# Softmax in sixteen-row tiles: three big buffers, one short buffer, and a changed order of divide and maximum

## The chip, the cores and the metric

The kernel runs on one core of a Trainium2 chip. The metric is the device time of one execution in microseconds; for the kernel before it is the median of 3 runs, 317.07 us (317.07 to 317.11). The core has several engines that run their own instruction streams and wait for each other by semaphores. Three of them matter here: the vector engine (DVE) for maxima and divisions, the scalar engine (ACT) for exponentials, and the transfers between main memory (HBM) and on-chip memory (SBUF), which 16 DMA engines carry. A transfer is issued by an instruction on one of three queues: SP's, POOL's (GpSimd's) or ACT's. SBUF has 128 partitions; a tile is a block of it, partitions by columns.

## The reference

A softmax with a temperature over the last axis of a 32 x 512 x 1024 float32 array; the temperature is 0.5.

```python
scaled = x / temperature
shifted = scaled - np.max(scaled, axis=-1, keepdims=True)
exp_x = np.exp(shifted)
return exp_x / np.sum(exp_x, axis=-1, keepdims=True)
```

There are 16,384 rows of 1024 numbers. With 128 partitions, that is 128 rows for each partition. In this text "a row" of a tile means one row of 1024 numbers in every partition: 128 x 4 KB, 0.524 MB. The whole task is 128 such rows in and 128 such rows out.

## The kernel before

A tile holds k consecutive rows in every partition and is loaded by one DMA, worked on in place and written back by one DMA from the same buffer. `PASSES` (line 10) lists the tiles, and in each tile the groups of rows that are worked on together: tile 0 has 12 rows in groups of 4, tiles 1 to 9 have 12 rows in groups of 6, tile 10 has 8 rows in groups of 4. The pool `data` has `BUFS` = 4 buffers of 12 rows (48 KB in each partition), so tile i uses the buffer of tile i-4.

A group is handled in three steps.

- `maximum` (lines 63 to 72): DVE reduces the group to one maximum for each row (L69) and scales it to a bias (L72).
- `exponential` (lines 74 to 85): ACT computes exp(scale * x + bias) row by row (L78), and each instruction also sums up its row.
- `divide` (lines 87 to 98): DVE takes the reciprocals of the sums (L90) and multiplies the group, either with one instruction on the whole group (L93, tiles 2, 3, 4, 6 and 8) or with one instruction for each row (L96, the other tiles).

`store` (lines 100 to 109) does something only after the last group of a tile: it issues the tile's store, on POOL's queue for tiles 0 to 5 and on ACT's for tiles 6 to 10, and then `load` issues the next load on SP's queue. That load waits until the store that last used its buffer has landed. Before the first store, POOL copies one number out of tile 2 (L106), so this store is not issued until tile 2 has been loaded.

The order on the engines is written by hand (lines 113 to 128). Four loads are issued first. Then, for each group g, the maximum and the exponentials of g come before the division of group g-1, so that ACT works while DVE divides the group before. This holds across tiles too: the last group of a tile is divided after the first maximum of the next tile. Only from tile 9 on (`ALONE`) does a tile's first group come after the division and the store of the tile before.

Of the kernel before, what the change touches and what calls it, by code (L numbers as in the profile page):

```python
# [1 line left out]

# [4 lines left out]

PASSES = [[4, 4, 4]] + [[6, 6]] * 9 + [[4, 4]]  # L10
BUFS = 4

WHOLE = (2, 3, 4, 6, 8)


BY_POOL = 6

ALONE = 9


@with_exitstack
def kernel(
    ctx: ExitStack,
    tc: tile.TileContext,
    x: bass.AP,
    temperature: bass.AP,
    out: bass.AP,
):
    nc = tc.nc
    f32 = mybir.dt.float32  # L30
    scale = 1.0 / float(temperature)
    extreme = mybir.AluOpType.max if scale > 0 else mybir.AluOpType.min

    P = 128
    xf = x.flatten_outer_dims()
    of = out.flatten_outer_dims()
    n, d = xf.shape
    rows = [sum(ks) for ks in PASSES]
    assert sum(rows) * P == n

    data = ctx.enter_context(tc.tile_pool(name="data", bufs=BUFS))
    stats = ctx.enter_context(tc.tile_pool(name="stats", bufs=4))


    groups = []
    for i, ks in enumerate(PASSES):
        for j, k in enumerate(ks):
            groups.append((i, sum(ks[:j]), k))

    def dram(t, i):  # L50
        block = t[P * sum(rows[:i]) : P * sum(rows[: i + 1]), :]
        return block.rearrange("(p k) d -> p k d", p=P, k=rows[i])

    tiles, small = [], []

    def load():
        i = len(tiles)
        if i < len(PASSES):
            xt = data.tile([P, rows[i], d], f32, name="xt")
            nc.sync.dma_start(out=xt, in_=dram(xf, i))  # L60
            tiles.append(xt)

    def maximum(g):
        i, a, k = groups[g]
        top, bias, sums, recip = (
            stats.tile([P, k], f32, name=name) for name in ("top", "bias", "sums", "recip")
        )
        small.append((bias, sums, recip))
        nc.vector.tensor_reduce(  # L69
            out=top, in_=tiles[i][:, a : a + k, :], axis=mybir.AxisListType.X, op=extreme  # L70
        )
        nc.vector.tensor_scalar_mul(bias, in0=top, scalar1=-scale)  # L72

    def exponential(g):
        i, a, k = groups[g]
        bias, sums, _ = small[g]
        for b in range(k):
            nc.scalar.activation(  # L78
                tiles[i][:, a + b, :],
                tiles[i][:, a + b, :],  # L80
                mybir.ActivationFunctionType.Exp,
                bias=bias[:, b : b + 1],
                scale=scale,
                accum_out=sums[:, b : b + 1],
            )

    def divide(g):
        i, a, k = groups[g]
        _, sums, recip = small[g]
        nc.vector.reciprocal(recip, sums)  # L90
        if i in WHOLE:
            xt = tiles[i][:, a : a + k, :]
            nc.vector.tensor_mul(xt, xt, recip.unsqueeze(2).to_broadcast([P, k, d]))  # L93
            return
        for b in range(k):
            nc.vector.tensor_scalar_mul(  # L96
                tiles[i][:, a + b, :], in0=tiles[i][:, a + b, :], scalar1=recip[:, b : b + 1]
            )

    def store(g):  # L100
        i, a, k = groups[g]
        if a + k == rows[i]:
            if i == 0:


                nc.gpsimd.tensor_copy(stats.tile([P, 1], f32, name="seen"), tiles[2][:, 0, 0:1])  # L106
            queue = nc.gpsimd if i < BY_POOL else nc.scalar
            queue.dma_start(out=dram(of, i), in_=tiles[i])  # L108
            load()

    with tc.manual_schedule():
        for _ in range(BUFS):
            load()
        for g in range(len(groups) + 1):

            alone = g < len(groups) and groups[g][0] >= ALONE and groups[g][1] == 0
            if g > 0 and alone:
                divide(g - 1)  # L120
                store(g - 1)
            if g < len(groups):
                maximum(g)
                exponential(g)
            if g > 0 and not alone:
                divide(g - 1)
                store(g - 1)


# [1 line left out]
_INS = ['x', 'temperature']  # L131
_OUTS = [((32, 512, 1024), 'float32')]

_NUMBERS = {'temperature': 0.5}


# [26 lines left out]
```

## Time and profile before

| what | value |
|---|---|
| median of 3 runs | 317.07 us |
| the profiled execution: its span | 315.8 us |
| DVE busy | 256.9 us (81%) |
| ACT busy | 148.3 us (47%) |
| POOL busy | 3.7 us (1%) |
| bytes read from and written to HBM | 67.11 MB each |
| mean rate over the span | 425 GB/s |
| loads: median time from issue to landing, 12 rows | 36.4 us |
| stores on POOL's queue, the same | 35.9 us |

The profile is of one execution. The span runs from the first to the last instruction that the profiler recorded; the device time holds a little more, 1.3 us here by the median. In groups of the profile, "L69" is the source line, "128x6 f32<-128x6144 f32" the output and input of one instruction (partitions by numbers), "x18" how often it ran; then come the total busy time, the mean of one in ns, and the idle time of the engine just before these instructions with what ended it. A DMA has two moments that matter: its issue on a queue, and its landing, when its semaphore tells the waiting engines that all bytes have arrived.

### The profile page before, as it was taken

To read this page: it belongs to the slowest core of one execution; us is meant where nothing else is said; L and a number is where in the kernel's file an instruction comes from. 1 tells how busy PE (TensorE), PEld (TensorE's weight loads), DVE (VectorE), ACT (ScalarE), POOL (GpSimd) and SP (SyncE) were. 2 spreads that over 40 slices of the span, in tenths; PEclk is the share of its full clock that TensorE was granted. 3 is DMA by queue.
4 is the path that set the end of the run, shared out by engine and by line. 5 is a ranking of instruction groups with operands and counts; after the bars stand their busy time and mean duration, and the time that the engine had idled before them with its cause. 6 is when DMAs were issued, how large, how long until landed. Compare 5 with 4: busy or idle time off the path is not lost.

```text
span 315.8 us, 525 instructions
## 1 busy us (share of the span) xinstructions
DVE 256.9 (81%) x147; ACT 148.3 (47%) x257; POOL 3.7 (1%) x11
## 2 busy tenths in 40 slices
DVE  0069999999999899979976994999199999969710
ACT  0029636775461807344471744074416802953700
POOL 0000001000000000000000000000000000000000
DMA  8999999999999999999999999999999999999996
GB/s 305 473 417 423 461 411 399 399 468 430 400 479 417 417 461 411 430 467 405 442 448 399 455 442 405 467 424 417 461 417 430 455 401 463 411 452 411 455 411 270
DMA packets 3171, 134.24 MB, mean 425 GB/s; under 512 B 352, under 2 KB 352, under 8 KB 352
## 3 DMA queue, kind: packets, MB, share of 16 engines
q1 hardware_dynamic: 1584, 67.11, 49.7%
q0 software_dynamic: 864, 37.75, 27.6%
q10 hardware_dynamic: 720, 29.36, 21.5%
q14 instruction: 3, 0.02, 0.0%
HBM read 67.11 MB, written 67.11 MB: 425 GB/s over the span
## 4 chain that ended last, share of the span: by engine, by line
DMA 47%; DVE 28%; ACT 11%; issue 9%; DVEq 0%; SPq 0%; POOLq 0%
DMA xt<-in_x_dram 25%; DMA out_dram<-xt 22%; DVE top L69 16%; ACT xt L78 11%; DVE xt L96 8%; DVE xt L93 2%; DVE bias L72 0%; DVE recip L90 0%; DVEq L158 0%; SPq L60 0%; POOLq L108 0%
## 5 line engine op out<-in xcount | busy, mean ns | idle before, releaser
L78 ACT ACTIVATE xt<-xt,bias 128x1024 f32<-128x1024 f32 x128 | 145.2, 1135 | 131.7 <-DVE recip L90 70.6
L69 DVE TENSOR_REDUCE top<-xt 128x6 f32<-128x6144 f32 (+1 forms) x23 | 139.9, 6083 | 37.8 <-DMA xt<-in_x_dram 37.8
L93 DVE TENSOR_TENSOR xt<-xt,recip 128x6144 f32<-128x6144 f32 x10 | 65.6, 6558 | 0.4
L96 DVE TENSOR_SCALAR xt<-xt,recip 128x1024 f32<-128x1024 f32 x68 | 46.2, 749 | 0.5
L78 ACT ACTIVATION_READ_ACCUMULATOR xt<-xt,bias 128x1 f32 x128 | 23.9, 187 | 0.0
L78 ACT ACT_TABLE_LOAD x1 | 1.3, 1283 | 18.3 <-DMA xt<-in_x_dram 18.3
L90 DVE RECIPROCAL recip<-sums 128x6 f32<-128x6 f32 (+1 forms) x23 | 4.2, 182 | 5.0 <-ACT xt L78 5.0
L108 POOL DMA_DIRECT2D out_dram<-xt x6 | 3.3, 554 | 129.6 <-ACT xt L78 82.7
L72 DVE TENSOR_SCALAR bias<-top 128x6 f32<-128x6 f32 (+1 forms) x23 | 3.9, 171 | 0.8
L106 POOL COPY seen<-xt 128x1 f32<-128x1 f32 x1 | 0.2, 185 | 46.9 <-DMA xt<-in_x_dram 46.9
L144 POOL MEMSET const-uint8-127<- 128x1 uint8 x1 | 0.1, 103 | 0.0
L144 POOL MEMSET const-bfloat16-1.0<- 128x1 bf16 x1 | 0.1, 102 | 0.0
L144 POOL MEMSET const-float32-0.0<- 128x1 f32 x1 | 0.1, 99 | 0.2 <-issue 0.2
L144 POOL MEMSET const-float32-1.0<- 128x1 f32 x1 | 0.1, 98 | 0.0
## 6 DMA issues: line engine op xcount, KB each, us to landing
xt<-in_x_dram SPq DMA_DIRECT2D x10, 6144.0 KB, 36.4
out_dram<-xt POOLq DMA_DIRECT2D x6, 6144.0 KB, 35.9
out_dram<-xt ACTq DMA_DIRECT2D x4, 6144.0 KB, 31.9
xt<-in_x_dram SPq DMA_DIRECT2D x1, 4096.0 KB, 34.9
out_dram<-xt ACTq DMA_DIRECT2D x1, 4096.0 KB, 13.5
```

The lines of the kernel that those rows point to most:

```text
L69: nc.vector.tensor_reduce(out=top, in_=tiles[i][:, a : a + k, :], axis=mybir.AxisListType.X, op=extreme)
L72: nc.vector.tensor_scalar_mul(bias, in0=top, scalar1=-scale)
L78: nc.scalar.activation(tiles[i][:, a + b, :], tiles[i][:, a + b, :], mybir.ActivationFunctionType.Exp, bias=bias[:, b : b + 1], scale=scal ...
L90: nc.vector.reciprocal(recip, sums)
L93: nc.vector.tensor_mul(xt, xt, recip.unsqueeze(2).to_broadcast([P, k, d]))
L96: nc.vector.tensor_scalar_mul(tiles[i][:, a + b, :], in0=tiles[i][:, a + b, :], scalar1=recip[:, b : b + 1])
L106: nc.gpsimd.tensor_copy(stats.tile([P, 1], f32, name="seen"), tiles[2][:, 0, 0:1])
L108: queue.dma_start(out=dram(of, i), in_=tiles[i])
L144: nc = _bacc.Bacc("TRN2", target_bir_lowering=False, num_devices=1)
```

## The change

All tiles change their size. Tile 0 has 3 rows; tiles 1 to 7 have 16 rows in four groups of 4; tile 8 has 3 rows; tile 9 has 10 rows in groups of 4, 3 and 3. That makes 10 loads and 10 stores where there were 11 of each.

The pool `data` has three buffers of 16 rows (64 KB in each partition); a second pool, `short`, has one buffer of 3 rows (12 KB), used by tile 0 and then by tile 8. Of the `data` buffers, tiles 1, 4 and 7 share the first, tiles 2, 5 and 9 the second, tiles 3 and 6 the third. The loads are issued in the order of `LOADS`: 0, 1, 2, 3, then 8, 4, 5, 6, 7, 9. So tile 8 is loaded as soon as the store of tile 0 has landed, long before it is worked on, and load 4 stands behind it on SP's queue.

Every division has one instruction for each row; the form for a whole group is gone. POOL's copy before the first store is gone. In every tile the first group now comes after the division and the store of the tile before: DVE divides the last group of a tile, and only then takes the first maximum of the next, for which it may have to wait for the load. Within a tile the order is as before. Stores of tiles 0 to 5 stay on POOL's queue, those of tiles 6 to 9 are on ACT's.

```diff
-PASSES = [[4, 4, 4]] + [[6, 6]] * 9 + [[4, 4]]
-BUFS = 4
-WHOLE = (2, 3, 4, 6, 8)
+PASSES = [[3]] + [[4, 4, 4, 4]] * 7 + [[3]] + [[4, 3, 3]]
+LOADS = [0, 1, 2, 3, 8, 4, 5, 6, 7, 9]
+BIG = 16
 BY_POOL = 6
-ALONE = 9
...
-    data = ctx.enter_context(tc.tile_pool(name="data", bufs=BUFS))
+    data = ctx.enter_context(tc.tile_pool(name="data", bufs=3))
+    short = ctx.enter_context(tc.tile_pool(name="short", bufs=1))
...
-    tiles, small = [], []
+    tiles, small = {}, []
+    todo = list(LOADS)
     def load():
-        i = len(tiles)
-        if i < len(PASSES):
-            xt = data.tile([P, rows[i], d], f32, name="xt")
-            nc.sync.dma_start(out=xt, in_=dram(xf, i))
-            tiles.append(xt)
+        if todo:
+            i = todo.pop(0)
+            if rows[i] <= 3:
+                xs = short.tile([P, rows[i], d], f32, name="xs")
+                tiles[i] = xs
+            else:
+                xt = data.tile([P, rows[i], d], f32, name="xt")
+                tiles[i] = xt
+            nc.sync.dma_start(out=tiles[i], in_=dram(xf, i))
...
         nc.vector.reciprocal(recip, sums)
-        if i in WHOLE:
-            xt = tiles[i][:, a : a + k, :]
-            nc.vector.tensor_mul(xt, xt, recip.unsqueeze(2).to_broadcast([P, k, d]))
-            return
         for b in range(k):
...
-        if a + k == rows[i]:
-            if i == 0:
-                nc.gpsimd.tensor_copy(stats.tile([P, 1], f32, name="seen"), tiles[2][:, 0, 0:1])
-            queue = nc.gpsimd if i < BY_POOL else nc.scalar
-            queue.dma_start(out=dram(of, i), in_=tiles[i])
-            load()
+        if a + k < rows[i]:
+            return
+        queue = nc.gpsimd if i < BY_POOL else nc.scalar
+        queue.dma_start(out=dram(of, i), in_=tiles[i])
+        load()
     with tc.manual_schedule():
-        for _ in range(BUFS):
+        for _ in range(4):
             load()
-        for g in range(len(groups) + 1):
-            alone = g < len(groups) and groups[g][0] >= ALONE and groups[g][1] == 0
-            if g > 0 and alone:
+        for g, (i, a, k) in enumerate(groups):
+            if g > 0 and a == 0:
                 divide(g - 1)
                 store(g - 1)
-            if g < len(groups):
-                maximum(g)
-                exponential(g)
-            if g > 0 and not alone:
+            maximum(g)
+            exponential(g)
+            if g > 0 and a > 0:
                 divide(g - 1)
                 store(g - 1)
+        divide(len(groups) - 1)
+        store(len(groups) - 1)
```

More of the change, by code (lines that the diff above doesn't have):

```diff
@@ L101, in store @@
         i, a, k = groups[g]
-        if a + k == rows[i]:
-            if i == 0:
-                nc.gpsimd.tensor_copy(stats.tile([P, 1], f32, name="seen"), tiles[2][:, 0, 0:1])
-            queue = nc.gpsimd if i < BY_POOL else nc.scalar
-            queue.dma_start(out=dram(of, i), in_=tiles[i])
-            load()
-    with tc.manual_schedule():
-        for _ in range(BUFS):
-            load()
-        for g in range(len(groups) + 1):
-            alone = g < len(groups) and groups[g][0] >= ALONE and groups[g][1] == 0
-            if g > 0 and alone:
+        if a + k < rows[i]:
[3 more added lines that the diff above has]
+        load()
+    with tc.manual_schedule():
+        for _ in range(4):
+            load()
+        for g, (i, a, k) in enumerate(groups):
+            if g > 0 and a == 0:
                 divide(g - 1)
                 store(g - 1)
-            if g < len(groups):
-                maximum(g)
-                exponential(g)
-            if g > 0 and not alone:
+            maximum(g)
+            exponential(g)
+            if g > 0 and a > 0:
                 divide(g - 1)
                 store(g - 1)
+        divide(len(groups) - 1)
+        store(len(groups) - 1)
 _INS = ['x', 'temperature']
```

## The prediction

> **What bounds the kernel now.** I read the strip of the page and its DMA queues first, then the windows, then the timeline of DVE.
>
> ```profile
> DVE  0069999999999899979976994999199999969710
> ACT  0029636775461807344471744074416802953700
> ...
> DMA  8999999999999999999999999999999999999996
> ...
> q1 hardware_dynamic: 1584, 67.11, 49.7%
> q0 software_dynamic: 864, 37.75, 27.6%
> q10 hardware_dynamic: 720, 29.36, 21.5%
> ```
>
> The DMA digits are 9 from the second slice to the last but one, and the queues add up to 98.8% of 16 engines' span: the transfers bound the kernel, DVE has dips. The packet records of the trace price a row: a packet of 48 KB (one partition of a 12-row tile) takes 1.815 us, an engine carries 8 of them one after the other, so a row costs 8 x 1.815 / 12 = 1.21 us one way and all 256, in and out, 309.8 us. The other 6.0 us of the span are: 1.76 before the first packet, 1.1 because the first packets took 2.9 us, 0.9 of pauses around the first store (52 to 57 us), 0.9 because the engines don't end together, and 1.2 from the last packet to the end. There is little to win; what can happen is that the engines run dry, when the next load waits for its buffer's store and no finished tile waits to be stored. The windows show today's margin:
>
> ```profile
> core 0: us, DVE busy (x) ACT busy (x) POOL busy (x), PEclk, DMA share, GB/s
> ...
> 140.00:169.00 29.00, 24.22 (x14) 13.80 (x24) 0.53 (x1) 1.00 1.00 432
> 169.00:198.00 29.00, 24.16 (x14) 13.80 (x24) 0.53 (x1) 1.00 1.00 432
> ...
> 303.00:315.80 12.80, 0.00 (x0) 0.00 (x0) 0.00 (x0) 1.00 0.77 332
> ```
>
> A stage of 29.0 us is one tile in and one out (24 x 1.21), at a DMA share of 1.00; packets of the load and the store alternate on each engine, so each runs at half speed. The tail from 303 is the last store alone, 8 rows. DVE's timeline of that last tile gives its prices:
>
> ```profile
> 284.52 4.41 DVE L69 TENSOR_REDUCE top<-xt 128x4 f32<-128x4096 f32 x1
> 288.96 0.17 DVE L72 TENSOR_SCALAR bias<-top 128x4 f32<-128x4 f32 x1
> 289.04 4.41 DVE L69 TENSOR_REDUCE top<-xt 128x4 f32<-128x4096 f32 x1
> 293.49 0.17 DVE L72 TENSOR_SCALAR bias<-top 128x4 f32<-128x4 f32 x1
> 293.84 0.18 DVE L90 RECIPROCAL recip<-sums 128x4 f32<-128x4 f32 x1 [0.18 <-ACT xt L78]
> 294.05 2.74 DVE L96 TENSOR_SCALAR xt<-xt,recip 128x1024 f32<-128x1024 f32 x4
> 298.36 0.18 DVE L90 RECIPROCAL recip<-sums 128x4 f32<-128x4 f32 x1 [1.57 <-ACT xt L78]
> 298.58 2.74 DVE L96 TENSOR_SCALAR xt<-xt,recip 128x1024 f32<-128x1024 f32 x4
> ```
>
> Two groups of 4 take 16.8 us (284.52 to 301.32). A group in the middle takes 7.38 us (30.45 to 37.83, maximum to maximum, DVE never idle).
>
> **The change part by part.**
>
> *Division by rows.* 60 rows go from L93 (6.558 / 6 = 1.093 us a row) to L96 (2.74 / 4 = 0.685): 24.5 us less for DVE. Worth nothing by itself while transfers set the pace; it shortens the tile times below.
>
> *Finish a tile first.* Before, a tile's last division stood behind the next tile's maximum: store 5 was issued at 179.94, although its last exponential ended at 166.9; in the new order it would be out at about 171.5 (0.2 + 4.1 + 0.3 later). The price is a wait at each tile's end: four exponentials take 4.6 us, the division beside them 3.0, so DVE waits some 1.6 (1.57 above) with the next maximum queued behind it, and ACT behind that. Nine such waits, 14 us, hidden where the next tile is not loaded yet, exposed from tile 7 on.
>
> *No copy on POOL.* Store 0 no longer waits for load 2 (46.9 us of idle POOL) and goes at about 17. Its 3.6 us on the engines only move to an earlier time. Two DMAs fewer: nothing, since packets follow each other without a pause. The early load of tile 8 is moved, too: 3.6 us, paid under the compute of tile 1.
>
> *Sixteen rows in three buffers.* Tile time on DVE: 16.8 + 2 x 7.38 = 31.6 us, 31.9 with 0.3 until the store is issued. A buffer's cycle is load 38.7 (32 x 1.21) + 31.9 + store 38.7 = 109.3, plus what lies between them. That was: last packet to landing 2.4 (load 5, 137.3 to 139.7) and 2.1 (store 2, 130.0 to 132.2), issue to first packet 7.1 (load 6) and 7.2 (store 3), of which most is waiting for a turn. These 12 us, larger still with packets of 64 KB (estimate 4/3 x 1.815 = 2.42 us each), bring the cycle to 121 or more, against three stages of 38.7, 116.1. Before, 29 + 29 + 40 (tile 5, landing 139.7 to store 179.9) and these 12 stood against four stages, 116. So the margin of some 6 is gone, and I follow the schedule:
>
> - Load 0 lands at 1.76 + 1.1 + 3 x 1.21 + 0.7, about 7.4. Store 0 goes at 17.2 (4-row group alone 12.3 us, 18.25 to 30.53; less 2.9 for a row; plus 0.3). Load 1 lands at about 28, with store 0 in its way for 2 us.
> - DVE: tile 1 until 60, tile 2 until 92, tile 3 until 124. Loads 0 to 3 and 8 and stores 0 and 1 are 73 rows, done at 73 x 1.21 + 3.8 = 92. Load 4 waits for the landing of store 1, and store 2 is issued at that same moment: the engines are dry for about 1.5 us (0.5 to land, 1.0 from issue to first packet, as at the start, 0.74 to 1.76). Before, this handover was covered by other loads.
> - Load 4 and store 2 share: landings at about 128 and 132. Tile 4 until 160. Load 5, behind store 2, shares with store 3 and lands at about 175: DVE idles some 15 us. Store 4 lands near 205, load 6 near 210. Load 7 is issued at 205, store 5 at about 208 (tile 5, 176 to 208).
> - When tile 7 lands, the engines have moved 118 rows of loads (all but tile 9), 67 rows of stores 0 to 4 and x rows of store 5: T7 = 5.8 + 1.21 (185 + x). 5.8 is 3.8 lost at the start, 1.5 at 92, 0.5 landing. x is bounded by 8 (store 5 comes late into the alternation) and 18 (all 16 and a packet of store 6): 239 to 251.5. I take 12, since load 7 is issued 3 us, a packet or so, before store 5: T7 = 244.2.
> - From there DVE sets the end: tile 7 31.6; tile 8 9.4 (12.3 - 2.9); tile 9 in 4, 3, 3: 21.6 (two maxima 8.0, wait for exponentials 1.3, division 2.9, maximum 3.4, division 2.2, wait for exponentials 1.5, division 2.3; 3 rows are 4 less 1.07 for the maximum, 1.14 on ACT, 0.68 to divide). Then store 9: 1.0 + 10 x 1.21 + 1.2 to the end = 14.3. Sum 76.9, with 0.3 for issues 77.2. Meanwhile stores 7 and 8 need only 23 us of the 31 that tiles 8 and 9 compute, and load 9 and store 6 are through at about 279: the engines run dry a second time, some 5 us, just before store 9.
>
> Span 244.2 + 77.2 = 321.4; the median lay 1.3 above the span: 322.7, and I say 323.
>
> The Trainium skill has a rule against this change (DMA: Bandwidth & Descriptors, Latency and other measured facts, on the HBM row pitch at large powers of two): 207 GB/s a direction at a pitch of 512 KiB against 214 when padded, less above. Here the pitch goes from 48 KB to 64 KB, below what it lists; were that loss to apply already, 240 rows would cost 3.4% more, an estimate of 10 us. This trace has 32 KB packets at a 32 KB pitch in its last tile: 1.213 us, 2/3 of 1.815 is 1.210, so by the row nothing is lost, and the sum above goes by the row.
>
> **The rivals.**
>
> *B, slower still.* Store 6, on a third queue, starts before load 7 is through, and takes turns from it: x = 18, T7 = 251.5, median 251.5 + 77.2 + 1.3 = 330. It decides where store 5 gets its packets in one turn earlier. For: load 7 would be through within a few us of store 6's issue (tile 6, 210 to 242). Against: load 7 has 3 us of a start.
>
> *C, not slower.* The transfers stay dense: the work is the same 256 rows, and with the same losses at both ends the time is 309.8 + 6.0 + 1.3 = 317.1. The place is tile 7's landing: it decides from T7 at or below 317.1 - 1.3 - 77.2 = 238.6, that is x below 8. For: a DMA share of 1.00 everywhere before, and stores released up to 8 us sooner. Against: load 7 then would have to pass store 5, where the packets alternated in every stage before.
>
> *D, slower packets.* 64 KB packets at a worse rate than 48 KB. The row at 32 KB gives 0.2% (0.7 us); twice or more the size, I bound it at 1%, 3 us: 326.
>
> **How the numbers follow.** Forecast 0.60 (319.5 to 326), B 0.24, C 0.10, D 0.06. The range takes in B: 319 to 331. A measurement of this kernel tells about 0.2% from no change, 316.4 to 317.7. C lies in that band, half of it a little below: faster 0.05, same 0.05, slower 0.90.
>
> **What would show it.** In the profile after: DVE idle some 15 us before one maximum near 160 to 176; DMA digits below 9 near 92 and in the last 15 us before the last store; each 16-row tile 31 to 32 us on DVE; the last store issued near 307 with a landing 14 us later. I am wrong if the DMA share stays near 99%, if tile 7 lands before 239, or if the packets of 64 KB don't take 2.42 us.

## The result: slower by 5%, and the profile after

The changed kernel takes 1.0508 times the time of the kernel before (95% interval 1.0471 to 1.0544); its runs lie between 332.99 and 340.77 us, the kernel before is at 317.07 to 317.11. Some executions of the changed kernel are disturbed and longer; the ratio leaves these out, and as the first profile is of one (339.74 us, span 338.0), a second profile of the same kernel, called the control here (337.50 us, span 335.7), stands beside it.

The page of the first profile, with the strips that answer to those of before:

```profile
span 338.0 us, 608 instructions
DVE 236.9 (70%) x227; ACT 148.9 (44%) x257; POOL 3.5 (1%) x10
...
DVE  1405997999799950099940699779973999758820
ACT  1400965285546630056630095509550666247600
...
DMA  8999999989899999999999999799999998898477
...
q1 hardware_dynamic: 1440, 67.11, 48.4%
q0 software_dynamic: 864, 43.52, 30.3%
q10 hardware_dynamic: 576, 23.59, 16.2%
```

DVE's work fell by 20 us (256.9 to 236.9), and the kernel became longer: DVE's total does not set the time. The DMA queues now fill 94.9% of the span instead of 98.8%, and the strip of the transfers has holes near the end (8477). The windows of the control (us from the span's start, then DVE, ACT and POOL busy, the granted clock, the DMA share and GB/s) put a place to them:

```profile
135.70:211.20 75.50, 56.66 (x56) 36.90 (x64) 1.07 (x2) 1.00 1.00 431
211.20:258.20 47.00, 29.55 (x28) 18.45 (x32) 0.00 (x0) 1.00 1.02 424
258.20:282.00 23.80, 23.37 (x17) 13.81 (x24) 0.00 (x0) 1.00 0.97 420
282.00:290.50 8.50, 6.49 (x13) 4.64 (x8) 0.00 (x0) 1.00 0.13 58
290.50:314.50 24.00, 18.92 (x16) 11.53 (x20) 0.00 (x0) 1.00 0.97 415
314.50:321.50 7.00, 5.15 (x10) 3.50 (x6) 0.00 (x0) 1.00 0.00 0
321.50:335.70 14.20, 0.00 (x0) 0.00 (x0) 0.00 (x0) 1.00 0.86 369
```

The transfers are dense to about 282, and then the engines are dry twice, 282 to 290.5 (share 0.13) and 314.5 to 321.5 (0.00), while DVE works through tiles 7, 8 and 9. Those two pauses, some 15 us, are most of the 20 by which the control's span exceeds the 315.8 of before. DVE's timeline of the control shows why it is late there; these are the maxima from tile 4 on that waited for a load, with the idle time before them in brackets:

```profile
133.24 4.42 DVE L71 TENSOR_REDUCE top<-xt 128x4 f32<-128x4096 f32 x1 [8.52 <-DMA xt<-in_x_dram]
178.24 4.42 DVE L71 TENSOR_REDUCE top<-xt 128x4 f32<-128x4096 f32 x1 [13.03 <-DMA xt<-in_x_dram]
213.65 4.42 DVE L71 TENSOR_REDUCE top<-xt 128x4 f32<-128x4096 f32 x1 [3.43 <-DMA xt<-in_x_dram]
258.23 4.42 DVE L71 TENSOR_REDUCE top<-xt 128x4 f32<-128x4096 f32 x1 [12.61 <-DMA xt<-in_x_dram]
```

Tiles 4, 5, 6 and 7 start here. Tile 7 landed at 258.2, where 244.2 was forecast. From there to the end the control takes 335.7 - 258.2 = 77.5 us, the first profile 338.0 - 260.5 = 77.5. The forecast for that part was 77.2, so the whole error lies ahead of tile 7's landing.

The first profile lost time in one more place, the stage of load 4 and store 2:

```profile
93.00:143.30 50.30, 29.42 (x29) 18.45 (x32) 1.06 (x2) 1.00 0.99 375
```

Here the engines are busy, a share of 0.99, but move 375 GB/s against 431 in a dense stage of the control: packets took a median of 2.9 us in load 4 instead of 2.418. The control's stage, 92.8 to 135.7, lasted 42.9 us instead of 50.3.

### The profile page after: what moved, and what is told of

Read it like the earlier page. It is cut to its first block, busy times and chain, and to the rows that moved or that the text cites. A ratio compares the mean times of both kernels' runs of the same rounds, so it can differ in the third digit from the quotient of the medians.

```text
span 338.0 us, 608 instructions
## 1 busy us (share of the span) xinstructions
DVE 236.9 (70%) x227; ACT 148.9 (44%) x257; POOL 3.5 (1%) x10
## 4 chain that ended last, share of the span: by engine, by line
DMA 58%; DVE 19%; issue 10%; ACT 9%; DVEq 0%; SPq 0%; ACTq 0%; POOLq 0%
DMA xt<-in_x_dram 35%; DMA out_dram<-xt 22%; DVE top L71 11%; ACT xt L80 8%; DVE xt L94 6%; ACT xs L80 1%; DVE xs L94 1%; DVE recip L92 1%; DVE bias L74 0%; DVEq L151 0%; SPq L63 0%; ACTq L80 0%; POOLq L103 0%
## 5 line engine op out<-in xcount | busy, mean ns | idle before, releaser
L80 ACT ACTIVATE xt<-xt,bias 128x1024 f32<-128x1024 f32 x122 | 138.5, 1136 | 156.4 <-DVE bias L74 100.3
L71 DVE TENSOR_REDUCE top<-xt 128x4 f32<-128x4096 f32 (+1 forms) x31 | 134.7, 4345 | 52.6 <-DMA xt<-in_x_dram 52.6
L94 DVE TENSOR_SCALAR xt<-xt,recip 128x1024 f32<-128x1024 f32 x122 | 83.7, 749 | 1.1
L92 DVE RECIPROCAL recip<-sums 128x4 f32<-128x4 f32 (+1 forms) x33 | 5.8, 175 | 24.8 <-ACT xt L80 17.6
L80 ACT ACTIVATION_READ_ACCUMULATOR xt<-xt,bias 128x1 f32 x122 | 22.7, 186 | 0.0
L71 DVE TENSOR_REDUCE top<-xs 128x3 f32<-128x3072 f32 x2 | 6.7, 3352 | 6.9 <-DMA xs<-in_x_dram 6.9
L80 ACT ACTIVATE xs<-xs,bias 128x1024 f32<-128x1024 f32 x6 | 6.8, 1137 | 8.8 <-DVE bias L74 8.8
L74 DVE TENSOR_SCALAR bias<-top 128x4 f32<-128x4 f32 (+1 forms) x33 | 5.6, 170 | 1.1
L94 DVE TENSOR_SCALAR xs<-xs,recip 128x1024 f32<-128x1024 f32 x6 | 4.2, 749 | 0.1
L80 ACT ACTIVATION_READ_ACCUMULATOR xs<-xs,bias 128x1 f32 x6 | 1.1, 187 | 0.0
```

The lines of the kernel that those rows point to most:

```text
L71: nc.vector.tensor_reduce(out=top, in_=tiles[i][:, a : a + k, :], axis=mybir.AxisListType.X, op=extreme)
L80: nc.scalar.activation(tiles[i][:, a + b, :], tiles[i][:, a + b, :], mybir.ActivationFunctionType.Exp, bias=bias[:, b : b + 1], scale=scal ...
L94: nc.vector.tensor_scalar_mul(tiles[i][:, a + b, :], in0=tiles[i][:, a + b, :], scalar1=recip[:, b : b + 1])
```

## The experiments

Ratios are to the kernel before on the same chip, with 95% intervals. The changed kernel itself, repeated as the control, gave 1.0564 (1.0500 to 1.0628) on a second chip, so its ratio is known to about 0.6%.

### Addresses: pitch125 and pitch128

The first question was why packets were slow after 93 us. `pitch125` keeps tiles, packets and schedule, and only changes which rows a partition owns:

```diff
     def dram(t, i):
-        block = t[P * sum(rows[:i]) : P * sum(rows[: i + 1]), :]
-        return block.rearrange("(p k) d -> p k d", p=P, k=rows[i])
+        if i == 0:
+            return t[: P * rows[0], :].rearrange("(p k) d -> p k d", p=P, k=rows[0])
+        rest = sum(rows[1:])
+        block = t[P * rows[0] :, :].rearrange("(p k) d -> p k d", p=P, k=rest)
+        at = sum(rows[1:i])
+        return block[:, at : at + rows[i], :]
```

> The changed kernel with another split of the rows over partitions: tiles 1 to 9 take their rows out of 125 consecutive rows that each partition now owns, so that neighbouring partitions lie 500 KB apart in HBM instead of 64 KB; packets stay 64 KB, the schedule stays. Theory A (the 64 KB packets of load 4 and store 2 are slow, 2.9 us and more instead of 2.42, because the 16 engines work in step on addresses a power of two apart): packets back to 2.42 us, load 4 lands near 128, tile 7 near 246, time 323 to 327, runs within 1 us of each other. Rival R (they are slow because load and store started together after all engines had run dry, whatever the addresses): as the changed kernel, 333 to 341.

Measured: 1.0534 (1.0466 to 1.0601), runs of 334.27 to 346.89. That is the changed kernel again, so theory A, addresses, falls as the cause of its time. Its profile had normal packets after 93 us and slow ones from 212 to 250 instead.

`pitch128` does the same with 128 rows, and all tiles.

> The same with all tiles out of 128 consecutive rows of each partition: partitions lie 512 KB apart, a power of two. Theory A: slow packets in more stages than before, 341 or more. Rival R: as the changed kernel, 333 to 341.

Measured: a median of 344.46, 338.56 to 355.61, and no ratio. That is near the 341 or more that theory A had expected here, and more of its stages had slow packets: in its profile packets took some 17 us an engine above the normal length, against 11 in the first profile of the changed kernel and 5.5 in the control. But outside the slow stages its packets of 64 KB took 2.418 us (the median), as with the other pitches. The Trainium skill (DMA: Bandwidth & Descriptors, Latency and other measured facts) reports 207 GB/s a direction at this pitch, against 214 with a padded one, 3.3% less, for copies between tensors in HBM. Outside the slow stages these packets show none of that. Whether a pitch of 512 KB makes slow stages more frequent was not settled.

### Three buffers alone: bufs3

```diff
-BUFS = 4
+BUFS = 3
```

on the kernel before, with 12-row tiles and the old order.

> The kernel before with three buffers instead of four, 12-row tiles and 48 KB packets kept. Following its schedule with packets of 1.815 us, each load waits for a store with nothing else queued: the engines run dry some 1.5 us at seven handovers and 7 us before the last store, 338. Theory A (addresses): packets stay at 1.815 us, 336 to 340. Rival R (restarts of load and store together slow packets): packets above 2 us after each restart, 343 or more.

Measured: 1.1164 (1.1088 to 1.1241), 357.8 us. The schedule's 338 and theory A's 336 to 340 were far too low; rival R's 343 or more held, without an upper bound. The windows show what the schedule had priced too low, each from one handover to the next:

```profile
97.00:131.00 34.00, 30.27 (x12) 15.34 (x27) 0.53 (x1) 1.00 0.92 370
131.00:165.00 34.00, 23.83 (x6) 12.26 (x22) 0.53 (x1) 1.00 0.91 370
```

A stage takes 34 us where 24 rows cost 29.0. A handover with nothing else queued thus costs 5 us, not 1.5: the engines are dry for 2 to 3 us, and the first packets of the load, up to 3.2 to 3.8 us long instead of 1.815, cost about 2 more. So slow first packets come with a restart by a load, also with 48 KB. Rival R's other half, slow packets long after the first ones, was seen at one of the seven loads that began on dry engines, load 9.

### The order of division and maximum: oldorder and finish

`oldorder` gives the changed kernel the order of before.

```diff
-            if g > 0 and a == 0:
-                divide(g - 1)
-                store(g - 1)
             maximum(g)
             exponential(g)
-            if g > 0 and a > 0:
+            if g > 0:
                 divide(g - 1)
                 store(g - 1)
```

> The changed kernel with the order of before: the last group of a tile is divided after the first maximum of the next. By schedule alone, with packets of 2.42 us, the engines run dry some 1.5 to 2 us at five handovers and not at the end: 324. Theory A: slow packets as in the changed kernel wherever load and store run in step, 334 to 345. Rival R: five restarts instead of two, each followed by slow packets, 345 or more. If finishing a tile first is what pays for the third buffer, it is slower than the changed kernel; if not, equal or faster.

Measured: 1.0561 (1.0519 to 1.0602), 335.51 to 336.77, the same as the changed kernel. Its windows, from one handover to the next:

```profile
92.40:134.70 42.30, 24.63 (x23) 15.98 (x28) 0.53 (x1) 1.00 0.95 397
134.70:177.40 42.70, 31.83 (x32) 18.85 (x33) 0.53 (x1) 1.00 0.95 393
177.40:220.00 42.60, 26.81 (x26) 18.25 (x32) 0.53 (x1) 1.00 0.96 394
```

Each stage takes 42.3 to 42.7 us, where 32 rows cost 38.7: five handovers at 3.6 to 4 us, instead of two pauses at the end. The time lies in theory A's range, but no stage was slow; the handovers, expected at 1.5 to 2 us, cost twice that. The new order wins nothing here and loses nothing; it moves the pauses. `finish` gives that order alone to the kernel before:

```diff
-ALONE = 9
+ALONE = 0
```

> The kernel before with the new order alone: every tile's last group is divided and stored before the next tile's first maximum (four buffers, 12-row tiles, all else as before). Theory: transfers already run without a pause, so stores that go up to 8 us sooner win nothing, and three groups' exposed waits cost little: 316 to 320. Rival F (the order itself opens pauses, because DVE waits for exponentials at each tile's end): 322 or more.

Measured: 1.0004 (0.9974 to 1.0034). With four buffers nothing waits for the stores that go out sooner:

```profile
111.00:260.00 149.00, 132.60 (x63) 72.71 (x128) 1.60 (x3) 1.00 1.00 434
```

### Slow packets: again, delay1, delay512, delay25, look3

In the profiles so far slow stages had one thing in common: their load and store were issued nearly at once. In the first profile of the changed kernel:

```profile
93.04 0.53 POOL L103 DMA_DIRECT2D out_dram<-xt  x1 [31.33 <-DVE xt L94]
93.10 0.33 SPq L63 DMA_DIRECT2D xt<-in_x_dram  x1
```

The next runs repeat the kernel and shift the stores by a copy on POOL.

> The changed kernel once more, as the control on the chip of the next two. In its profile store 2 and load 4 were issued 0.06 us apart (93.04 and 93.10) and the stage after them ran at 375 GB/s. Theory C (a load and a store issued within some 0.1 us of each other on dry engines keep the engines in step, and packets stay slow for the whole transfer): profiles in which the two are that close show packets of 2.9 us and more until both are through, others don't; runs from 333 to 341. Rival R (every restart slows packets, whatever the order): slow packets for a whole transfer in every run.

```diff
+        if i == 2:
+            late = stats.tile([P, 1], f32, name="late", bufs=1)
+            nc.gpsimd.tensor_copy(late, tiles[i][:, rows[i] - 1, d - 1 : d])
         queue = nc.gpsimd if i < BY_POOL else nc.scalar
```

> The changed kernel with a copy of one column of tile 2's last row on POOL ahead of store 2, which puts that store some 0.6 us later, after load 4 instead of beside it. Theory C: packets of 2.42 us after the first one, load 4 lands some 8 us earlier than at 143, all runs near the fast ones of the changed kernel, 330 to 334. Rival R: no difference, 333 to 341.

`delay512` copies 512 columns instead of one, and `delay25` does that ahead of stores 2 and 5.

> The same with a copy of 512 columns, which puts store 2 a further 0.5 to 2 us later. Theory C: as with one column, 330 to 334. Rival R: 333 to 341 and the delay on top.

> The changed kernel with POOL's copy of 512 columns ahead of stores 2 and 5, which puts both about 0.6 us later against loads 4 and 7. Theory C (load and store issued within some 0.1 us of each other keep all packets slow): neither pair is that close, all runs within 1% of each other, 332 to 336. Rival: some runs at 338 and more, as in the control.

> The changed kernel, one more look. Theory C: packets stay slow after a handover only if its load and store were issued within 0.15 us of each other (so far: 0.06, 0.03, 0.14 and 0.02 us apart with slow stages, 0.31 and more apart without).

Measured: again 1.0564 (1.0500 to 1.0628); delay1 1.0544 (1.0479 to 1.0608); delay512 1.0492 (1.0439 to 1.0545); delay25 1.0519 (1.0465 to 1.0573), with one run at 341.8; look3 one time, 333.92. No ratio differs from the changed kernel's, and the runs scatter as widely as its own: up to 342.80 in again, 345.54 in delay1, 338.88 in delay512, against the 330 to 334 expected of theory C. The one-column copy did not delay the store at all: it went out 0.27 us after DVE began the next maximum (92.38 and 92.65), without a copy 0.37 after (92.77 and 93.14 in the control); the large copy put it 0.70 after (92.48 and 93.18), 0.3 us later. In the profiles, the four stages whose load and store were issued 0.02 to 0.14 us apart had slow packets well beyond the first ones (the first profile, pitch128 at 93, pitch125 at 211, bufs3 at 266), and none of those 0.26 or more apart did, but for a part of one in pitch128 at 0.49. So the closeness and the slow stages go together, and theory C is neither refuted by a profile nor shown: no run forced the two issues together, and the run of 341.8 with both stores shifted has no profile, so a shift of 0.3 us doesn't rule a close pair out there. It does not carry the result: in the control no stage was slow, and it is 5% longer than before.

### What delays tile 7: pool7, gate5, hold5

The packet records, counted up to tile 7's landing, split the landing into rows and loss:

| profile | tile 7 lands | x, rows of stores 5 and 6 moved | loss = landing - 1.21 (185 + x) |
|---|---|---|---|
| forecast | 244.2 | 12 | 5.8 |
| control (again) | 258.2 | 20.8 | 9.2 |
| look3 | 254.6 | 19.2 | 7.5 |
| first profile | 260.5 | 15.4 | 18.0 |

Where no stage was slow, in the control and look3, the larger part of the error is x. `pool7` takes store 6 off the third queue.

```diff
-BY_POOL = 6
+BY_POOL = 7
```

> The changed kernel with store 6 on POOL's queue behind store 5, so that no third queue takes turns with load 7. The control's profile has load 7 and store 5 issued at 211, store 6 at 245.6 on ACT's queue, tile 7 landing at 258.2, and 77.5 us from there to the end. Theory B (the third queue delays load 7, some 4 rows of store 6 moved before it landed): tile 7 lands 3 to 6 us earlier, near 253, and the end follows it one to one, 329 to 332. Rival (store 5 alone, moved whole beside load 7, makes the delay): landing and time as in the control, 333 to 337.

Measured: 1.0511 (1.0473 to 1.0549), tile 7 at 253.7, with x = 17.4: all 16 rows of store 5, and 1.4 of store 6, which had 4.8 in the control and 3.2 in look3. So the third queue accounts for 2 to 3 of the 7 to 9 rows above the forecast, worth 2 to 4 us. The landing is what theory B expected, but also near look3's with the third queue in use; the median, 334.06, is its rival's, and no gain can be told from the changed kernel. The larger part is store 5, which goes through whole beside load 7. `gate5` takes store 5 away from there, and `hold5` shifts it by 12 copies of 512 columns on POOL, from 210.5 in the control to 218.2:

```diff
# gate5
+        if i == 5:
+            nc.gpsimd.tensor_copy(stats.tile([P, 1], f32, name="seen"), tiles[7][:, 0, 0:1])
# hold5
+        if i == 5:
+            late = stats.tile([P, 512], f32, name="late", bufs=1)
+            for b in range(12):
+                nc.gpsimd.tensor_copy(late, tiles[i][:, rows[i] - 1, d - 512 : d])
```

> The changed kernel with store 5 held back until tile 7 has landed (POOL reads one number of tile 7 first, as the kernel before did with tile 2). Theory X (the 16 rows of store 5 and the first of store 6, moved turn by turn with load 7, are what puts tile 7's landing at 254 to 258 instead of 244): tile 7 lands near 235. Load 9 then waits for store 5, whose buffer it takes, and lands late, so the end follows only in part: 326 to 331. Rival Y (load 7 is late by itself, by restarts and slow packets): tile 7 lands at 248 or later, time 333 or more.

> The changed kernel with store 5 held back by some 7 us of copies on POOL, so that it begins behind load 7. Theory X: x falls to about 12 rows, tile 7 lands near 246 and load 9 is not late yet: 323 to 329, faster than the changed kernel by holding a store back. Rival Y: 333 or more.

Measured: in hold5 tile 7 lands at 246.7 with x = 11.1 and a loss of 9.4, and the time is 1.0377 (1.0311 to 1.0444), 328.64 to 331.62, a little above the 323 to 329 expected. The interval lies wholly below the changed kernel's: holding a store back by nearly 8 us makes this kernel 1.2 to 1.8% faster, by its two ratios. In gate5 tile 7 lands at 232.7 with x = 0 and a loss of 8.8. Theory X holds: landing = loss + 1.21 (185 + x), with a loss of 7.3 to 9.4 in all eight profiles of this order without a slow stage, x being 0, 11, and 17 to 21 in the other six (control, look3, pool7 and the three delays).

But gate5's time is 1.0659 (1.0567 to 1.0751), 335.95 to 341.11 against 326 to 331 expected. Its chain of waits (start, duration, what) shows what came instead:

```profile
233.23 25.90 DMA out_dram<-xt
259.13 0.02 SPq L63
259.15 0.03 issue
259.18 38.72 DMA xt<-in_x_dram
297.90 0.02 issue
297.92 4.43 DVE top L71
```

Store 5, held until 233.2, lands at 259.1; only then may load 9 take its buffer, and tile 9 starts at 297.9 instead of 299.5 in the control, although tile 7 had landed 25 us earlier. I had put that price too low: load 9 shares with stores 6 and 7 for 38.7 us. Nor could DVE use the whole 25 us. It had tile 6 until 245.3, 12.6 us after tile 7 had landed; the first maximum of tile 7 follows then, without a wait:

```profile
245.29 4.42 DVE L71 TENSOR_REDUCE top<-xt 128x4 f32<-128x4096 f32 x1
```

hold5 has load 9 next in line, too, only shorter:

```profile
218.15 40.57 DMA out_dram<-xt
...
258.86 34.57 DMA xt<-in_x_dram
293.43 0.02 issue
293.46 4.43 DVE top L71
```

So in both, what puts load 7 ahead puts load 9 behind, because load 9 needs the buffer of the store that was held back.

### Something better: allact

With finish at 1.0004, the remaining loss that can be named in the kernel before is the 0.9 us around its first store.

```diff
-BY_POOL = 6
+BY_POOL = 0
```

> The kernel before with every store on ACT's queue. In its profile packets around the first store, on POOL's queue, lost 0.9 us. Theory: the loss is that queue's first use, and goes: 316.0 to 316.4. Rival: it comes with any first store into running loads, 317.0 to 317.3; or ACT, held up by waiting for divisions, delays exponentials: 318 or more.

Measured: 1.0021 (1.0009 to 1.0032). The loss is still there (1.3 us an engine between 40 and 60), so it is not POOL's queue, and the kernel is 0.2% slower. No version here beats the kernel before.

## Why the prediction was wrong

The forecast was slower, and it is: the mechanism, three buffers without a margin, so that the engines run dry, is what the profiles show, and bufs3, which takes away one buffer and nothing else, shows it alone. The range was too low: 319 to 331, and 317.09 x 1.0508 is 333.2. Step by step:

- *Work on the engines.* Right. Packets of 64 KB take 2.418 us (forecast 2.42), so rival D, slower packets, did not come true outside the slow stages, and a dense stage of 16-row tiles runs at 431 GB/s, as before.
- *DVE.* Right in its times: DVE's work fell by 20 us net. No run here changes the form of the division alone, so "worth nothing by itself" is not shown. A tile was to take 31.9 us from landing to store; in the control tile 5 takes 32.3 (178.2 to 210.5).
- *Finish a tile first, costed at nothing where transfers bind.* Right: 1.0004 alone.
- *The tail, 77.2 us from tile 7's landing.* Right: 77.5 in both profiles. Two pauses were in it, not one: besides the one before store 9 (forecast some 5 us, 7 measured), 8 us before store 7, because tile 7 was later than forecast while load 9 and store 6 were done at the forecast time (282 against 279).
- *The handover at 92, "dry for about 1.5 us".* Mis-sized. In the control the engines lost 1.9 us dry and 1.6 in slow first packets, 3.5 in all; oldorder's handovers cost 3.6 to 4, bufs3's 5. The first load of the kernel before had shown the second part, packets of 2.9 instead of 1.8 us; I charged it once, at the start, and not at a restart.
- *"I take 12, since load 7 is issued 3 us, a packet or so, before store 5."* This is the step that failed. In the control the order was the other way round:

```profile
210.51 0.53 POOL L103 DMA_DIRECT2D out_dram<-xt  x1 [44.47 <-DVE xt L94]
211.21 0.33 SPq L63 DMA_DIRECT2D xt<-in_x_dram  x1
```

So it is in look3, pool7, delay1, delay512 and delay25, with store 5 ahead by 0.4 to 2.4 us. Store 5 came 2.5 us later than forecast (208), load 7 6 us later (205), because it waits for store 4, which landed at 211.2. The control's chain of waits (start, duration, what) has the two one after the other:

```profile
165.51 45.65 DMA out_dram<-xt
211.16 0.02 SPq L63
211.18 0.03 issue
211.21 46.99 DMA xt<-in_x_dram
```

Stores 2 and 4 landed 3.7 and 6 us late (135.7 and 211.2, forecast 132 and 205), loads 5 and 6 only 3 to 4 (178.2 and 213.6), so load 7 fell back behind store 5. Store 5 then went through whole, and some 4 rows of store 6 with it: x = 19 to 21 instead of 12, 9 to 11 us. With 2 to 3 us more loss (9.2 and 7.5 instead of 5.8), that is the whole difference of 10 to 14 us at tile 7's landing. gate5 and hold5, which set x to 0 and 11, moved the landing by just these rows. The lead itself was also worth less than I took it for: in the first profile load 7 was 1.7 us ahead (219.48 and 221.19), as forecast in kind, and x was 15.4; in hold5 it was 7.2 us ahead, and x was 11.1. By these two, x = 12 needs a lead of some 6 us, an estimate, not 3.
- *Rival B* came nearest, with a landing at 251.5. Store 5 went through whole, as it said, and store 6 took 3 to 5 rows on a third queue before tile 7 landed. But the third queue was the smaller part (pool7: 2 to 3 rows, and no gain in time that shows), and its bound x = 18 and its loss of 5.8 were both too small, so that the range's upper end, built on it, was 2 us short of the time.
- *Rival C* asked for a landing by 238.6. gate5 reached 232.7 and still was slow: its condition was incomplete, as load 9 decides then. It also left out DVE, which has tile 6 until 245.3; the prediction's own "tile 6, 210 to 242" stood against a start at 238.6, and against the lower bound of 239, which was thus worth no more than 242.
- *The three signs of being wrong* (a DMA share near 99%, a landing before 239, packets of another length) did not appear. They guarded against rivals C and D; no sign was named for a landing that is too late.
- *Two small slips.* The 0.9 us around the first store of the kernel before are not pauses: between 50 and 60 us its engines are idle for 0.01 us, and packets of load 3 took longer. And of the 256 rows 224 move in packets of 64 KB, not 240, which makes the 10 us estimated for the pitch 9.

## What to carry to other kernels

A kernel bound by transfers, as this one is, lives on having the next transfer queued before the last one ends. Bigger tiles in fewer buffers keep the bytes and take that reserve away; then price a handover by a restart of the engines (here 3 to 5 us), not by the latency of one transfer. Where a load and a store take turns, count the store's rows into the load's landing: here all 16 with the store issued up to 2.4 us ahead, 14 of them with it 1.7 us behind, 11 with it 7 us behind. And before you pull a load forward, see whether the engine that needs it is free by then, and which later load pays.

## What was not expected of the hardware

- First packets of a load after engines had run dry are slow: for load 4 a median of 3.1 to 3.9 us over the first sixteen instead of 2.418 (64 KB), and of 2.5 to 2.6 instead of 1.815 in bufs3 (48 KB), but for its slow stage. Dryness alone does not do it: store 7, alone after the pause of 282 to 290.5 in the control, began with packets of 2.45 us, and store 5 of gate5, alone as well, did too. In delay1, where store 2 went out 0.3 us ahead of load 4, its first packets took 3.1. Why is open.
- A whole stage can run slow at a DMA share of 0.99 (375 GB/s over 50 us against 416 over the same stage of the control). Such packets were seen in four stages whose load and store were issued 0.02 to 0.14 us apart, and in a part of one at 0.49. The cause stays open.
- A one-column copy on POOL ahead of a store cost nothing: 0.27 us from DVE's next maximum to the store with it, 0.37 without. One of 512 columns, 0.61 us long, cost 0.33. The 0.6 us that the kernel before showed between its copy (47.31) and its store (47.89) was thus no price of the copy.
